# Pairs: one 512-column matmul over both halves of x1, parts added by SBUF-to-SBUF transfers, loop in written order, convolution set back

## The chip, the core and the metric

The kernel runs on one core of one Trainium2 chip. The metric is the device time of one execution in microseconds; a time is a median of runs. One profiled execution of the kernel before gives the rows below.

## What is computed

One decoder layer in fp32, sequence 512, width 2048: a token mixer (an RG-LRU group and a differential-attention group over one input projection), an output projection, a LayerNorm, and a gated MLP with a width-3 causal convolution, again with a LayerNorm. The part that the change touches is the MLP, whose up projection has 2 x 5632 columns:

```python
x = _layernorm(DEEPNORM_ALPHA * x + mix, ln_mix_g[i], ln_mix_b[i])
hu = _causal_dwconv(jnp.einsum('bsd,df->bsf', x, w_up[i]), ffn_conv_w[i], ffn_conv_b[i])
g, u = jnp.split(hu, 2, axis=-1)
ffn = jnp.einsum('bsf,fd->bsd', jax.nn.gelu(g) * u, w_down[i])
x = _layernorm(DEEPNORM_ALPHA * x + ffn, ln_ffn_g[i], ln_ffn_b[i])
```

## The kernel before

**Numbers.** Every fp32 operand of a large product is split into a high and a low fp32r part (`split`, L101 to L107: ScalarE copies the high part, L105; VectorE subtracts, L106). A product is three matmuls into one PSUM bank: weight high by x high, weight high by x low, weight low by x high (`mm3`, L109 to L114). Weights stand still, activations of 256 or 512 columns move; in w_down the hidden parts stand still and 512 columns of weights move.

**Stages.** Projections, attention and RG-LRU run to about 500 us, the output projection to 677 us. The first LayerNorm and the first four up tiles run together (`up_first`) to about 745 us: x1, the normalized input, is kept as tiles [hi | lo] of 256 + 256 columns, one for each half of the tokens and each of 16 k-tiles. Two more up tiles (i = 2, 3) are computed plainly to 797.4 us; beside them x1 is turned and stored (`turned`) and the sums of x1 for the pairs are made (`forms`, subtractions on POOL, splits on ScalarE and VectorE). Then come 40 **pairs** to 1603.6 us, then **w_down** in chunks of hidden tiles (`CHUNKS`), each added to an accumulator in SBUF, and the last chunk with the final LayerNorm.

**A pair** (class `Pair`, L772 to L873) computes one gate tile cg and one up tile cu, 128 rows by 512 tokens each, as a 2 by 2 block product with seven products instead of eight, in the order of `PRODUCTS`: p1, p5, p6, p2, p7, p3, p4. A product has 8 k-tiles and so 24 matmuls of 256 columns. p1, p6, p7 and p4 add up in bank x, p5 and p3 in y, p2 in z. The pair's steps are numbered in products from its own first one:

- `before`, steps -6 to 4: SP loads the raw weights r21, r11, r12, r22 (512 KB each); POOL issues DMAs that add another block onto r21 and r11 (`onto`, L785); VectorE makes and changes the sum s2 (L805, L816); each product's weights are split two steps ahead, into three buffers.
- `early`, steps 1 to 7: ScalarE copies a bank out (L840, L843, L845, L850, L855), VectorE adds a bank onto what was copied (L847, L852, L853).
- `late`, steps 6 to 12: `tap` (ScalarE, L759), `conv` (VectorE, L753), Gelu (L867), the product of gate and up (L871) and the store of the hidden tile to `hidd` in DRAM, which w_down loads back as `hid`.

**Order.** The loop at L931 calls for each product k the steps early, before, late and product of all pairs that are due; the Tile scheduler then orders the instructions of each engine by priority and readiness as it sees them. Each engine runs its own queue in order; DMAs wait on the queue of the engine that issues them (SP for loads and stores, POOL for the adding ones). Large tiles (x1, forms, kept weights, cg, cu, accumulators, hid) share one pool of 62 buffers of 128 x 512 (`A_BUFS`); conv and sq tiles have 12 (`T_BUFS`), raws 6.

Of the kernel before, what the change touches and what calls it, by code (L numbers as in the profile page):

```python
# [16 lines left out]
P = 128  # L17
# [7 lines left out]
QB = S // P  # L25
DFF = 5632
FT = DFF // P
CHUNKS = [20, 20, 4]
ALPHA = 2.0 ** 0.25
LN_EPS = 1e-5  # L30
RMS_EPS = 1e-5
# [14 lines left out]
NC_ = C_LQ + 4 * DH  # L46


A_BUFS = 62
T_BUFS = 12  # L50
RAW_BUFS = 3
RAW_UP = 6
# [19 lines left out]
def f32(ap):  # L72
    return ap.bitcast(F32)
# [3 lines left out]
def trunk_kernel(ctx, tc, xT, w_qkg, w_v, gate_w, w_out0, w_out, w_up0, w_up, w_down, ln2, consts, out):  # L77
# [202 lines left out]
    def v_proj(n):  # L280
        pv = [bank() for _ in range(QB)]
        if n == 0:
            load_x(0)
            W.load(1)
            load_x(1)
            W.load(2)
            load_x(2)
            load_x(3)
            W.load(3)
        for unit in range(KT // 2):  # L290
            if n == 0:
                x[2 * unit] = split(x[2 * unit])
            parts = W.take()
            if n + unit == 0:
                parts += W.take()
            if n == 0:
                x[2 * unit + 1] = split(x[2 * unit + 1])
                load_x(2 * unit + 4)
                load_x(2 * unit + 5)
            for i in range(2):  # L300
                kt = 2 * unit + i
                for tt in range(QB):
                    xs = [z[:, tt * P : (tt + 1) * P] for z in x[kt]]
                    mm3(pv[tt], xs, parts[i], kt == 0, kt == KT - 1)
                tick(4 * TK)
            if n == 0 and unit == 0:
                nc.sync.dma_start(cst, consts)
            if n == 0 and unit == 4:
                constants()
        for tt in range(QB):  # L310
            vt[tt] = split(pv[tt])

    def proj():

# [305 lines left out]
    for dt in range(KT):  # L620

        if dt == 3:
            W.hold = True
        if W.hold and not W.raws:
            assert not side
            early.close()
            W.pool = ctx.enter_context(tc.tile_pool(name="rawu", bufs=1))
            W.bufs, W.hold = RAW_UP, False
            W.load()
        xr = t_tile(F32, "xr")  # L630
        nc.sync.dma_start(xr, xT[dt])
        xrs.append(xr)
        if dt == 0:
            continue
        if dt == 1:
            pair = [bank(), bank()]
            for u in range(KT // 4):
                parts = W.take()
                for kk in range(4):
                    i = 4 * u + kk  # L640
                    tick(2 * TK)
                    assert ms[i] is not None
                    hi, lo = parts[kk // 2]
                    for o in range(2):
                        c = slice((kk % 2 * 2 + o) * P, (kk % 2 * 2 + o + 1) * P)
                        mm3(pair[o], (hi[:, c], lo[:, c]), ms[i], i == 0, i == KT - 1)
            for o in range(2):
                residual(o, pair[o])
            continue
        if dt >= KT - 2:  # L650
            wl.append([W.take(), W.take()])
            ys.append(a_tile(F32, "y"))
# [66 lines left out]
    def forms(j):  # L719
        a, b = ys[j], ys[j + KT // 2]  # L720
        sub = nc.gpsimd.tensor_tensor
        t14, t23 = t_tile(F32, "t14"), t_tile(F32, "t23")
        (t1, t4), (t2, t3) = sides(t14), sides(t23)
        (b11, b12), (b21, b22) = sides(a), sides(b)
        sub(t1, b12, b11, ALU.subtract)
        sub(t2, t1, b22, ALU.subtract)
        sub(t4, t2, b21, ALU.add)
        sub(t3, b22, b12, ALU.subtract)
        h14, l14 = a_tile(F32R, "hi"), a_tile(F32R, "lo")
        nc.scalar.activation(h14, t14, AF.Copy, scale=-1.0)  # L730
        nc.vector.scalar_tensor_tensor(l14, t14, -1.0, f32(h14), ALU.mult, ALU.subtract)
        h23, l23 = split(t23)
        form["p1", j], form["p2", j] = sides(x1[j][0]), sides(x1[j + KT // 2][0])
        form["p3", j] = sides(x1[j + KT // 2][1])
        form["p5", j], form["p4", j] = zip(sides(h14), sides(l14))
        form["p6", j], form["p7", j] = zip(sides(h23), sides(l23))

    def turned(kt):

# [32 lines left out]
    class Pair:  # L772
# [61 lines left out]

        def early(self, at):
            copy, add = nc.scalar.activation, nc.vector.tensor_tensor
            a, b = slice(0, HALF), slice(HALF, S)
            if at == 1:
                self.cg = a_tile(F32, "cg")
                copy(self.cg[:, a], self.x, AF.Copy)  # L840
            elif at == 2:
                self.p5 = t_tile(F32, "p5")[:, :HALF]
                copy(self.p5, self.y, AF.Copy)  # L843
            elif at == 3:
                copy(self.cg[:, b], self.x, AF.Copy)  # L845
            elif at == 4:
                add(self.cg[:, a], self.cg[:, a], self.z, ALU.add)  # L847
            elif at == 5:
                self.cu = a_tile(F32, "cu")
                copy(self.cu[:, b], self.x, AF.Copy, scale=-1.0)  # L850
            elif at == 6:
                add(self.cg[:, b], self.cg[:, b], self.y, ALU.add)  # L852
                add(self.cu[:, b], self.cu[:, b], self.p5, ALU.subtract)  # L853
            elif at == 7:
                copy(self.cu[:, a], self.x, AF.Copy, scale=-1.0)  # L855

        def late(self, at):
            if at == 6:
                self.g = tap(self.cg, 2 * self.i)
                conv(self.g, self.cg, 2 * self.i, 1)  # L860
            elif at == 7:
                conv(self.g, self.cg, 2 * self.i, 2)
                self.u = tap(self.cu, 2 * self.i + 1)
            elif at == 8:
                conv(self.u, self.cu, 2 * self.i + 1, 1)
            elif at == 9:
                nc.scalar.activation(self.g, self.g, AF.Gelu_apprx_tanh)  # L867
            elif at == 10:
                conv(self.u, self.cu, 2 * self.i + 1, 2)
            elif at == 11:  # L870
                nc.vector.tensor_tensor(self.g, self.g, self.u, ALU.mult)  # L871
            elif at == 12:
                nc.sync.dma_start(hidd[self.i], self.g)  # L873

    pairs = [Pair(i) for i in range(PLAIN, FT)]
# [53 lines left out]
            hid[i] = split(t)  # L929

    last = NP * len(pairs)  # L931
    for k in range(last):
        step(k, "early", 1, 8)
        step(k, "before", -6, 5)
        step(k, "late", 6, 13)
        step(k, "product", 0, NP)
        ready({last - 5: 4, last - 3: 12, last - 2: 16}.get(k, 0))
        if k == last - 4:
            W.load()
    for k in range(last, last + 6):  # L940
        step(k, "early", 1, 8)
        step(k, "late", 6, 13)

    acc = {}
    at = 0
# [28 lines left out]
        at += n  # L974


    ready(FT)
    for tt in range(QB):
        tok = slice(tt * P, (tt + 1) * P)
# [14 lines left out]
        os = []  # L994
        for fb in range(NF):
            y = acc[tt, fb]
            sq = t_tile(F32, "sq")
            nc.scalar.activation(
                sq, y, AF.Square, bias=nmean, accum_out=square[:, fb : fb + 1]
            )  # L1000
            os.append(a_tile(F32, "o"))
# [94 lines left out]
```

## Time and profile before

| | |
|---|---|
| median of 3 runs | 2094.55 us (2094.19 to 2094.75) |
| profiled execution, its own time | 2095.22 us |
| its span, first to last instruction | 2093.4 us |
| mean granted TensorE clock | 0.996 of full speed |
| busy share of the span: TensorE, VectorE, ScalarE, POOL | 99%, 62%, 48%, 9% |
| the 40 pairs | 797.4 to 1603.6 us, 20.16 us each |

The span is what the trace covers; the execution's own time is 1.8 us longer. A row of the page's engine part gives busy us, share of the span and number of instructions. Matmuls are pipelined, so their records overlap: their pace is the distance of starts. PE is TensorE, PEld its weight loads, DVE VectorE, ACT ScalarE, POOL GpSimd, SP the engine that issues most DMAs.

### The profile page before, as it was taken

The numbers are of one execution on the slowest core, as the hardware profiler recorded it, in microseconds if no ns is written. First come the engines' busy times: TensorE is split into PE (matmuls) and PEld (weight loads), VectorE is DVE, ScalarE is ACT, GpSimd is POOL, SyncE is SP. The second block draws the span as 40 slices with busy tenths as digits, with TensorE's granted clock in tenths as the row PEclk, the third lists the DMA queues.
The fourth block names the chain that finished last, engine by engine and source line by source line (L and its number), as shares of the span: only waits on it lengthen the run. The fifth ranks groups of instructions, "written<-read, shape, count | busy, mean of one in ns | idle before, by whom it ended". The sixth has DMA issues, their size and how long they took to land.

```text
span 2093.4 us, 32163 instructions
## 1 busy us (share of the span) xinstructions
PE 2075.2 (99%) x12889; PEld 1876.3 (90%) x12889; DVE 1303.3 (62%) x1963; ACT 997.2 (48%) x1635; POOL 182.5 (9%) x227
## 2 busy tenths in 40 slices
PE   9999999999999999999999999999999999999997
PEld 7888888888888899999999999999999888888886
DVE  6566645777334957777777777787778323422346
ACT  4475736667223745555555555555556222322232
POOL 1000000000222233010110100101010000000000
PEclk9999999999999999999999999999999999999999
DMA  6222222222433246666656666666667723522222
GB/s 218 96 78 89 81 91 76 86 91 92 152 114 126 94 124 165 173 170 174 171 164 174 168 174 171 165 175 166 172 172 255 257 92 114 171 91 101 96 95 81
DMA packets 98166, 288.72 MB, mean 138 GB/s; under 512 B 10208, under 2 KB 18400, under 8 KB 98016
## 3 DMA queue, kind: packets, MB, share of 16 engines
q1 hardware_dynamic: 86496, 244.71, 34.2%
q0 software_dynamic: 11520, 41.95, 11.1%
q8 instruction: 101, 1.65, 0.3%
q14 instruction: 49, 0.40, 0.1%
HBM read 266.70 MB, written 19.92 MB: 137 GB/s over the span
## 4 chain that ended last, share of the span: by engine, by line
PE 95%; ACT 3%; DVE 2%; issue 0%; DMA 0%; DVEq 0%; SPq 0%; ACTq 0%
PE ps L112 93%; PE ps L341 1%; PE ps L342 0%; ACT gt L450 0%; PE ps L743 0%; DVE y L603 0%; PE ps L371 0%; ACT s L353 0%; ACT a L456 0%; ACT L468 0%; ACT L456 0%; ACT L450 0%; ACT L353 0%; DVE hh L472 0%; ACT gt L458 0%
## 5 line engine op out<-in xcount | busy, mean ns | idle before, releaser
L105 ACT ACTIVATE whi<-raw 128x512 fp32r<-128x512 f32 (+1 forms) x676 | 528.1, 804 | 836.8 <-PE ps L112 747.8
L106 DVE TENSOR_TENSOR wlo<-raw,whi 128x512 fp32r<-128x512 f32 (+1 forms) x676 | 606.8, 915 | 474.9 <-ACT whi L105 472.5
L112 PE MATMUL ps<-hi,whi 128*128 128x256 f32 (+1 forms) x2048 | 661.2, 323 | 0.0
L112 PE MATMUL ps<-hi,wlo 128*128 128x256 f32 (+1 forms) x2048 | 658.9, 322 | 1.2 <-DVE wlo L106 1.2
L112 PE MATMUL ps<-lo,whi 128*128 128x256 f32 (+1 forms) x2048 | 658.4, 322 | 0.0
L112 PEld LDWEIGHTS ps<-hi,wlo 128*128 128x128 f32 x2048 | 390.1, 190 | 31.2 <-DVE wlo L106 2.4
L112 PEld LDWEIGHTS ps<-hi,whi 128*128 128x128 f32 x2048 | 390.1, 190 | 27.8 <-ACT cu L850 0.3
L112 PEld LDWEIGHTS ps<-lo,whi 128*128 128x128 f32 x2048 | 390.2, 191 | 27.5 <-issue 0.2
L112 PE MATMUL ps<-x,whi 128*128 128x256 f32 x2176 | 398.0, 283 | 0.0
L112 PEld LDWEIGHTS ps<-x,whi 128*128 128x128 f32 x2176 | 339.5, 192 | 0.0
L112 PE MATMUL ps<-x,wlo 128*128 128x256 f32 x1088 | 307.9, 283 | 0.0
L112 PE MATMUL ps<-whi,hi 128*128 128x512 f32 x768 | 299.6, 390 | 0.1
L112 PE MATMUL ps<-wlo,hi 128*128 128x512 f32 x768 | 299.4, 390 | 0.0
L112 PE MATMUL ps<-whi,lo 128*128 128x512 f32 x768 | 299.1, 390 | 0.0
L112 PEld LDWEIGHTS ps<-x,wlo 128*128 128x128 f32 x1088 | 208.8, 192 | 0.0
L112 PEld LDWEIGHTS ps<-whi,hi 128*128 128x128 f32 x768 | 144.5, 188 | 30.9 <-ACT hi L105 0.9
L112 PEld LDWEIGHTS ps<-wlo,hi 128*128 128x128 f32 x768 | 144.5, 188 | 29.9
L112 PEld LDWEIGHTS ps<-whi,lo 128*128 128x128 f32 x768 | 144.4, 188 | 29.9
L785 POOL DMA_DIRECT2D raw<-in_w_up x80 | 70.5, 1010 | 758.2 <-DMA raw<-in_w_up 637.8
L753 DVE SCALAR_TENSOR_TENSOR cv<-cg,cst,cv 128x511 f32<-128x511 f32 x80 | 59.8, 747 | 1.4
L753 DVE SCALAR_TENSOR_TENSOR cv<-cu,cst,cv 128x511 f32<-128x511 f32 x80 | 59.5, 744 | 0.0
L112 PE MATMUL ps<-x,hi 128*128 128x256 f32 x256 | 49.6, 295 | 4.6 <-DVE x L106 2.8
(196 smaller groups left out, 1768.6 us busy)
## 6 DMA issues: line engine op xcount, KB each, us to landing
raw<-in_w_up SPq DMA_DIRECT2D x176, 512.0 KB, 3.8
raw<-in_w_down SPq DMA_DIRECT2D x88, 512.0 KB, 3.3
raw<-in_w_up POOLq DMA_DIRECT2D x80, 512.0 KB, 6.3
raw<-in_w_qkg SPq DMA_DIRECT2D x64, 512.0 KB, 3.5
raw<-in_w_out SPq DMA_DIRECT2D x32, 512.0 KB, 3.6
hidd<-cv SPq DMA_DIRECT2D x44, 256.0 KB, 4.0
hid<-hidd SPq DMA_DIRECT2D x44, 256.0 KB, 5.6
raw<-in_w_v SPq DMA_DIRECT2D x15, 512.0 KB, 4.5
```

What stands on the lines that cost most here:

```text
L105: nc.scalar.activation(hi, src, AF.Copy)
L106: nc.vector.tensor_tensor(lo, src, f32(hi), ALU.subtract)
L112: nc.tensor.matmul(ps, a, b, start=first and n == 0, stop=last and n == 2, skip_group_check=onto)
L341: nc.tensor.matmul(ps[:, :L], qs, k[c][:, :L], start=True, stop=False)
L753: nc.vector.scalar_tensor_tensor(t[:, d:], src[:, : S - d], col(C_FW + 3 * ti + 2 - d), t[:, d:], ALU.mult, ALU.add)
L785: nc.gpsimd.dma_start(self.raw[name], w_up[2 * (self.i - 2) + g][:, n * 1024 : (n + 1) * 1024], accum_op=ALU.add,)
```

## The change

- **Products.** `mm2` replaces `mm3` in the pairs: one matmul of the high weight over the whole tile [hi | lo], 512 columns into the whole bank, and one of the low weight over hi, 256 columns into the bank's first half; on a product's last k-tile in the other order. A bank so holds two parts, which are yet to be added.
- **Results.** The copies and adds of `early` cover both parts (128 x 2 x 256). cg and cu are tiles of 128 x 1024 from a ring of 4 (`c_tile`), and POOL issues one DMA for each that adds its second half onto the first, SBUF to SBUF, 256 KB.
- **Late steps** move from 6 to 12 to 10 to 18.
- **Order.** The loop stands under `tc.manual_schedule()`, which keeps the written order on every engine, and the calls are early, late, before, product.
- **Forms.** Each product gets its own tile [hi | lo]; the splits are of 256 columns, 8 instead of 4 for each j.
- **Buffers.** `A_BUFS` 62 to 56, `CHUNKS` [20, 20, 4] to [12, 12, 16, 4]; the lo parts of v, the last two y and the final LayerNorm's o move to other pools.

```diff
-CHUNKS = [20, 20, 4]
+CHUNKS = [12, 12, 16, 4]
-A_BUFS = 62
+A_BUFS = 56
+    def c_tile(name):
+        return W.pool.tile([P, 2 * S], F32, tag="c", bufs=4, name=name)
+    def mm2(ps, w, x, first, last, onto=False):
+        n = ps.shape[-1] // 2
+        steps = [(ps, w[0], x), (ps[:, :n], w[1], x[:, :n])]
+        for k, (o, a, b) in enumerate(reversed(steps) if last else steps):
+            nc.tensor.matmul(
+                o, a, b, start=first and k == 0, stop=last and k == 1, skip_group_check=onto
+            )
...
-        h14, l14 = a_tile(F32R, "hi"), a_tile(F32R, "lo")
-        nc.scalar.activation(h14, t14, AF.Copy, scale=-1.0)
-        nc.vector.scalar_tensor_tensor(l14, t14, -1.0, f32(h14), ALU.mult, ALU.subtract)
-        h23, l23 = split(t23)
...
+        for name, t in (("p5", t1), ("p4", t4)):
+            z = form[name, j] = a_tile(F32R, "hl")
+            hi, lo = sides(z)
+            nc.scalar.activation(hi, t, AF.Copy, scale=-1.0)
+            nc.vector.scalar_tensor_tensor(lo, t, -1.0, f32(hi), ALU.mult, ALU.subtract)
+        for name, t in (("p6", t2), ("p7", t3)):
+            form[name, j] = a_tile(F32R, "hl")
+            split(t, *sides(form[name, j]))
...
-                self.x, self.y, self.z = [bank()[:, :HALF] for _ in range(3)]
+                self.x, self.y, self.z = bank(), bank(), bank()
...
-                mm3(ps, (hi[:, c], lo[:, c]), form[name, j], new and j == 0, j == n - 1, not new)
+                mm2(ps, (hi[:, c], lo[:, c]), form[name, j], new and j == 0, j == n - 1, not new)
...
             elif at == 6:
-                add(self.cg[:, b], self.cg[:, b], self.y, ALU.add)
-                add(self.cu[:, b], self.cu[:, b], self.p5, ALU.subtract)
+                add(self.g2[:, :, b], self.g2[:, :, b], y, ALU.add)
+                nc.gpsimd.dma_start(self.cg[:, :S], self.cg[:, S:], accum_op=ALU.add)
+                add(self.u2[:, :, b], self.u2[:, :, b], self.p5, ALU.subtract)
             elif at == 7:
-                copy(self.cu[:, a], self.x, AF.Copy, scale=-1.0)
+                copy(self.u2[:, :, a], x, AF.Copy, scale=-1.0)
+                nc.gpsimd.dma_start(self.cu[:, :S], self.cu[:, S:], accum_op=ALU.add)
 
         def late(self, at):
-            if at == 6:
-                self.g = tap(self.cg, 2 * self.i)
+            if at == 10:
+                self.g = tap(self.cg[:, :S], 2 * self.i)
+            elif at == 11:
                 conv(self.g, self.cg, 2 * self.i, 1)
...
-    for k in range(last):
-        step(k, "early", 1, 8)
-        step(k, "before", -6, 5)
-        step(k, "late", 6, 13)
-        step(k, "product", 0, NP)
...
+    with tc.manual_schedule():
+        for k in range(last):
+            step(k, "early", 1, 8)
+            step(k, "late", 10, 19)
+            step(k, "before", -6, 5)
+            step(k, "product", 0, NP)
+            ready({last - 5: 4, last - 3: 12, last - 2: 16}.get(k, 0))
```

What the instructions of three engines look like in their queues follows; line numbers of the changed kernel are its own.

TensorE, the start of a p5 product, before (hi and lo are the parts of a form, whi and wlo those of the weight, ps the bank):

```order
L112 MATMUL ps_16233<-hi_6700,whi_16191 128x256
L112 MATMUL ps_16233<-lo_6701,whi_16191 128x256
L112 MATMUL ps_16233<-hi_6700,wlo_16192 128x256
L112 MATMUL ps_16233<-hi_6786,whi_16191 128x256
L112 MATMUL ps_16233<-lo_6787,whi_16191 128x256
L112 MATMUL ps_16233<-hi_6786,wlo_16192 128x256
```

TensorE, the same place in a pair of the changed kernel, from the end of p1 on (hl is the form's tile of both parts):

```order
L125 MATMUL ps_12586<-x1_6472,wlo_12607 128x256
L125 MATMUL ps_12586<-x1_6472,whi_12606 128x512
L125 MATMUL ps_12584<-hl_6708,whi_12632 128x512
L125 MATMUL ps_12584<-hl_6708,wlo_12633 128x256
L125 MATMUL ps_12584<-hl_6798,whi_12632 128x512
L125 MATMUL ps_12584<-hl_6798,wlo_12633 128x256
```

Two matmuls stand where three stood, and the last k-tile of a product ends with its wide one.

VectorE, from one r21 + r11 sum (L805) on, before (wlo is a weight's low part, cv a convolution's tile):

```order
L805 TENSOR_TENSOR raw<-raw 128x1024
L106 TENSOR_TENSOR wlo<-raw,whi 128x1024
L847 TENSOR_TENSOR cg<-cg,ps 128x256
L106 TENSOR_TENSOR wlo<-raw,whi 128x1024 x2
L853 TENSOR_TENSOR cu<-cu,p_12315 128x256
L852 TENSOR_TENSOR cg<-cg,ps 128x256
L106 TENSOR_TENSOR wlo<-raw,whi 128x1024
L753 SCALAR_TENSOR_TENSOR cv<-cg,cst,cv 128x511
L753 SCALAR_TENSOR_TENSOR cv<-cg,cst,cv 128x510
L106 TENSOR_TENSOR wlo<-raw,whi 128x1024
L816 TENSOR_TENSOR raw<-raw 128x1024
L753 SCALAR_TENSOR_TENSOR cv<-cu,cst,cv 128x511
```

VectorE, the same place in the changed kernel (L823 is that sum, L109 the low part, L771 the convolution):

```order
L823 TENSOR_TENSOR raw<-raw 128x1024
L875 TENSOR_TENSOR cg<-cg,ps 128x2x256
L877 TENSOR_TENSOR cu<-cu,p_11189 128x2x256
L109 TENSOR_TENSOR wlo<-raw,whi 128x1024
L771 SCALAR_TENSOR_TENSOR cv<-cu,cst,cv 128x511
L109 TENSOR_TENSOR wlo<-raw,whi 128x1024
L771 SCALAR_TENSOR_TENSOR cv<-cu,cst,cv 128x510
L109 TENSOR_TENSOR wlo<-raw,whi 128x1024
L834 TENSOR_TENSOR raw<-raw 128x1024
L109 TENSOR_TENSOR wlo<-raw,whi 128x1024
L897 TENSOR_TENSOR cv<-cv 128x512
```

The convolution of cu (L771) that stands behind the adds onto cg and cu is now that of the pair before, with weight splits between.

POOL, two pairs of the changed kernel (L803 is the adding load that was L785; before, POOL's queue held only rows of L785 in the pairs):

```order
L876 DMA cg<-cg 128x512
L880 DMA cu<-cu 128x512
L803 DMA raw<-in_w_up 128x1024 x2
L876 DMA cg<-cg 128x512
L880 DMA cu<-cu 128x512
L803 DMA raw<-in_w_up 128x1024 x2
```

The transfers of cg and cu stand between a pair's r11 and the next r21.

## Rows read from the trace of the kernel before

**Rows 1.** The page: busy time, share of the span and instructions; the chain by engine.
```profile
PE 2075.2 (99%) x12889; PEld 1876.3 (90%) x12889; DVE 1303.3 (62%) x1963; ACT 997.2 (48%) x1635; POOL 182.5 (9%) x227
...
PE 95%; ACT 3%; DVE 2%; issue 0%; DMA 0%; DVEq 0%; SPq 0%; ACTq 0%
```

**Rows 2.** The chain in order of time: start us, us, what.
```profile
697.00 3.37 DVE y L603 x5
...
797.37 1285.29 PE ps L112 x8832
```

**Rows 3.** PE's timeline in a pair: start us, duration us, instruction.
```profile
999.75 0.28 PE L112 MATMUL ps<-x,wlo 128*128 128x256 f32 x1
999.87 0.40 PE L112 MATMUL ps<-x,whi 128*128 128x256 f32 x2
1000.11 0.28 PE L112 MATMUL ps<-x,wlo 128*128 128x256 f32 x1
```

**Rows 4.** Windows: us busy (x started) of each engine, PEclk, DMA share, GB/s.
```profile
1000.00:1100.00 100.00, 100.00 (x836) 100.00 (x835) 77.18 (x85) 52.70 (x75) 8.74 (x10) 1.00 0.64 170
...
1700.00:1800.00 100.00, 100.00 (x443) 82.81 (x442) 35.87 (x55) 27.60 (x48) 0.00 (x0) 1.00 0.39 125
```

**Rows 5.** PE's timeline in w_down: start us, duration us, instruction.
```profile
1849.91 0.39 PE L112 MATMUL ps<-whi,hi 128*128 128x512 f32 x1
...
1850.82 0.39 PE L112 MATMUL ps<-wlo,hi 128*128 128x512 f32 x1
```

**Rows 6.** Groups by form, 820 to 1590 us, then 1620 to 2050, then 744 to 797: busy us, mean ns.
```profile
L106 DVE TENSOR_TENSOR wlo<-raw,whi 128x1024 fp32r<-128x1024 f32 x267 | 326.9, 1224 | 130.9 <-ACT whi L105 129.8
...
L816 DVE TENSOR_TENSOR raw<-raw 128x1024 f32<-128x1024 f32 x39 | 47.8, 1225 | 1.3
...
L753 DVE SCALAR_TENSOR_TENSOR cv<-cu,cst,cv 128x511 f32<-128x511 f32 x39 | 29.0, 745 | 0.0
...
L871 DVE TENSOR_TENSOR cv<-cv 128x512 f32<-128x512 f32 x39 | 27.0, 692 | 1.3
...
L847 DVE TENSOR_TENSOR cg<-cg,ps 128x256 f32<-128x256 f32 x38 | 16.0, 422 | 25.9 <-PE ps L112 25.9
...
L853 DVE TENSOR_TENSOR cu<-cu,p 128x256 f32<-128x256 f32 x38 | 15.9, 418 | 0.0
L840 ACT ACTIVATE cg<-ps 128x256 f32<-128x256 f32 x39 | 14.3, 366 | 0.0
...
L967 DVE TENSOR_TENSOR acc<-acc,ps 128x512 f32<-128x512 f32 x32 | 21.6, 687 | 13.6 <-PE ps L112 13.6
...
L745 ACT ACTIVATE x1t<-ps 128x512 f32<-128x512 f32 x14 | 7.6, 584 | 0.0
```

**Rows 7.** POOL's timeline, 1190 to 1262 us: start us, us, instruction, idle before.
```profile
1197.32 1.75 POOL L785 DMA_DIRECT2D raw<-in_w_up  x2 [18.41 <-DMA raw<-in_w_up]
...
1257.80 0.86 POOL L785 DMA_DIRECT2D raw<-in_w_up  x1 [18.41 <-DMA raw<-in_w_up]
1259.31 0.86 POOL L785 DMA_DIRECT2D raw<-in_w_up  x1 [0.65 <-issue]
```

**Rows 8.** DMAs of 900 to 1560 us: line 785's landing; its queue's packets, MB, share of 16 engines.
```profile
DMA to landing us min/median/max: 5.0/7.1/10.3
...
q0 software_dynamic: 9331, 33.96, 28.6%
```

**Rows 9.** Timelines of ScalarE and VectorE at the start of the pairs.
```profile
798.99 0.64 ACT L730 ACTIVATE hi<-t 128x512 fp32r<-128x512 f32 x1
...
800.22 0.69 DVE L731 SCALAR_TENSOR_TENSOR lo<-t,hi 128x512 fp32r<-128x512 f32 x1
...
801.49 0.68 DVE L106 TENSOR_TENSOR lo<-t,hi 128x512 fp32r<-128x512 f32 x1
```

**Rows 10.** What PE's weight loads waited for, 690 to 2080 us: us, times, longest.
```profile
PEld ps L112 <- ACT cu L850: 0.3, 1, 0.3
```

**Rows 11.** Groups by form on VectorE, 677 to 709 us: busy us, mean ns.
```profile
L106 DVE TENSOR_TENSOR lo<-raw,hi 128x512 fp32r<-128x512 f32 x9 | 6.7, 744 | 0.0
```

More of the change, by code (lines that the diff above doesn't have):

```diff
@@ L310, in v_proj @@
         for tt in range(QB):
-            vt[tt] = split(pv[tt])
+            vl = att.tile([P, S], F32R, tag="vl", bufs=6, name="vl")
+            vt[tt] = split(pv[tt], lo=vl)
     def proj():
@@ L651, in trunk_kernel @@
             wl.append([W.take(), W.take()])
-            ys.append(a_tile(F32, "y"))
+            if dt == KT - 2:
+                last2 = c_tile("y")
+            ys.append(last2[:, :S] if dt == KT - 2 else last2[:, S:])
             continue
@@ L728, in forms @@
         sub(t3, b22, b12, ALU.subtract)
-        h14, l14 = a_tile(F32R, "hi"), a_tile(F32R, "lo")
-        nc.scalar.activation(h14, t14, AF.Copy, scale=-1.0)
-        nc.vector.scalar_tensor_tensor(l14, t14, -1.0, f32(h14), ALU.mult, ALU.subtract)
-        h23, l23 = split(t23)
[L733 to L736, printed above, removed]
+        form["p1", j], form["p2", j] = x1[j][0], x1[j + KT // 2][0]
+        form["p3", j] = x1[j + KT // 2][1]
+        for name, t in (("p5", t1), ("p4", t4)):
[6 more added lines that the diff above has]
+            split(t, *sides(form[name, j]))
     def turned(kt):
@@ L832, in product @@
                 c = slice(j * P, (j + 1) * P)
-                mm3(ps, (hi[:, c], lo[:, c]), form[name, j], new and j == 0, j == n - 1, not new)
+                mm2(ps, (hi[:, c], lo[:, c]), form[name, j], new and j == 0, j == n - 1, not new)
         def early(self, at):
+            two = lambda z: z.rearrange("p (z t) -> p z t", z=2)
             copy, add = nc.scalar.activation, nc.vector.tensor_tensor
             a, b = slice(0, HALF), slice(HALF, S)
+            x, y, z = [two(k) for k in (self.x, self.y, self.z)]
@@ L838, in early @@
             if at == 1:
-                self.cg = a_tile(F32, "cg")
-                copy(self.cg[:, a], self.x, AF.Copy)
+                self.cg = c_tile("cg")
+                self.g2 = two(self.cg)
+                copy(self.g2[:, :, a], x, AF.Copy)
             elif at == 2:
-                self.p5 = t_tile(F32, "p5")[:, :HALF]
-                copy(self.p5, self.y, AF.Copy)
+                self.p5 = two(t_tile(F32, "p5"))
+                copy(self.p5, y, AF.Copy)
             elif at == 3:
-                copy(self.cg[:, b], self.x, AF.Copy)
+                copy(self.g2[:, :, b], x, AF.Copy)
@@ L846, in early @@
             elif at == 4:
-                add(self.cg[:, a], self.cg[:, a], self.z, ALU.add)
+                add(self.g2[:, :, a], self.g2[:, :, a], z, ALU.add)
             elif at == 5:
-                self.cu = a_tile(F32, "cu")
-                copy(self.cu[:, b], self.x, AF.Copy, scale=-1.0)
+                self.cu = c_tile("cu")
+                self.u2 = two(self.cu)
+                copy(self.u2[:, :, b], x, AF.Copy, scale=-1.0)
             elif at == 6:
-                add(self.cg[:, b], self.cg[:, b], self.y, ALU.add)
@@ L857, in late @@
         def late(self, at):
-            if at == 6:
-                self.g = tap(self.cg, 2 * self.i)
+            if at == 10:
+                self.g = tap(self.cg[:, :S], 2 * self.i)
+            elif at == 11:
                 conv(self.g, self.cg, 2 * self.i, 1)
-            elif at == 7:
+            elif at == 12:
                 conv(self.g, self.cg, 2 * self.i, 2)
-                self.u = tap(self.cu, 2 * self.i + 1)
-            elif at == 8:
+            elif at == 13:
+                nc.scalar.activation(self.g, self.g, AF.Gelu_apprx_tanh)
+                self.u = tap(self.cu[:, :S], 2 * self.i + 1)
+            elif at == 14:
@@ L865, in late @@
                 conv(self.u, self.cu, 2 * self.i + 1, 1)
-            elif at == 9:
-                nc.scalar.activation(self.g, self.g, AF.Gelu_apprx_tanh)
-            elif at == 10:
+            elif at == 15:
                 conv(self.u, self.cu, 2 * self.i + 1, 2)
-            elif at == 11:
+            elif at == 17:
                 nc.vector.tensor_tensor(self.g, self.g, self.u, ALU.mult)
-            elif at == 12:
+            elif at == 18:
                 nc.sync.dma_start(hidd[self.i], self.g)
@@ L931, in trunk_kernel @@
     last = NP * len(pairs)
-    for k in range(last):
-        step(k, "early", 1, 8)
-        step(k, "before", -6, 5)
-        step(k, "late", 6, 13)
-        step(k, "product", 0, NP)
[L937 to L940, printed above, removed]
-        step(k, "early", 1, 8)
-        step(k, "late", 6, 13)
+    with tc.manual_schedule():
[5 more added lines that the diff above has]
+            ready({last - 5: 4, last - 3: 12, last - 2: 16}.get(k, 0))
+            if k == last - 4:
+                W.load()
+    for k in range(last, last + 12):
+        step(k, "early", 1, 8)
+        step(k, "late", 10, 19)
     acc = {}
@@ L974, in trunk_kernel, with split2 @@
         at += n
+    def split2(z):
+        return z[:, :S], z[:, S:]
     ready(FT)
@@ L993, in trunk_kernel @@
         nc.vector.tensor_scalar_mul(nmean, nmean, -1.0 / D)
-        os = []
+        os = [z for _ in range(NF // 2) for z in split2(c_tile("o"))]
         for fb in range(NF):
@@ L1000, in trunk_kernel @@
             )
-            os.append(a_tile(F32, "o"))
             nc.vector.scalar_tensor_tensor(os[fb], y, nmean, gb[0][fb], ALU.add, ALU.mult)
```

## The prediction

> **What bounds the kernel now.** Read the page's first part first: TensorE is busy for 99% of the span and carries 95% of the chain that ended last [rows 1]. Busy matmuls overlap in the records, so that share alone does not prove a limit. The chain in order of time does: from 797.37 us one unbroken piece of 8832 matmuls runs for 1285 us, through all pairs and nearly all of w_down, and ahead of it the stretch around the first LayerNorm has VectorE pieces [rows 2]. So in the pairs the time is the number of matmuls times the pace at which they start. For the pace read the timeline, starts and not durations (a 283 ns record overlaps the next two): three 256-column matmuls of one k-tile take 1000.11 - 999.75 = 0.36 us [rows 3]. The windows confirm it: 836 start in 100 us, one per 0.1197 us, while w_down's 512-column ones come 443 in 100 us, one per 0.226 us, both at clock 1.00 [rows 4]; 1850.82 - 1849.91 is four of these, 0.2275 us each [rows 5]. I take 0.120 and 0.2264 us (1285.29 us = 6720 x 0.120 + 2112 x 0.2264 + 0.7 fits both). Next to TensorE, VectorE is at 77% and ScalarE at 53% in this stretch [rows 4].
>
> **The products.** Per pair, product and k-tile, 40 x 7 x 8 = 2240 times, three 256-column matmuls become one of 512 and one of 256. The first moving tile holds [hi|lo], so the columns are the same 768. By the rows: before 3 x 0.120 = 0.360 us, after 0.2264 + 0.120 = 0.3464 us, a gain of 13.6 ns, and 2240 x 13.6 ns = **-30.5 us**, all of it on the path. A pair goes from 20.16 to 19.40 us, a product from 2.88 to 2.77 us. What no row shows is a 256 behind a 512 with another weight. Bounds: at the 256's price per column the triple stays at 0.360 (gain 0); at the 512's price per column it is 1.5 x 0.2264 = 0.3396 (gain 45.7 us). I take the sum of the two rows, since both leave the same 13 ns over columns / 2.4 GHz (106.7 and 213.3 ns), so that the excess goes by the matmul. The Trainium skill, page "TensorE: Matmul & The Clock Gate", section "Wait — 56ns, not 53.3ns?", speaks against so much: it gives a warm matmul only about 2.5 ns over its columns, by which one matmul fewer would be worth 2240 x 2.5 ns = 5.6 us; the trace disagrees, with 13 ns at both widths.
>
> **Work added beside it.** Three VectorE adds per pair go from 256 to 512 columns: 422, 422 and 418 ns become about 687, 687 and 692 ns (the widest analogues) [rows 6], +0.80 us. Five ScalarE copies go from 366 to 584 ns, +1.09 us [rows 6]. VectorE then has 0.77 x 20.16 + 0.80 = 16.4 us per 19.40 us (84%), ScalarE 0.53 x 20.16 + 1.09 = 11.7 us (60%). In totals both stay covered by TensorE; if the cover went, they would cost up to 40 x 1.9 = 76 us. The bank's reuse is the closest edge: p1, p6, p7 and p4 add up in one bank, and each is copied out (0.58 us now) during the one product, 2.77 us, that stands before the next of them. In-order VectorE: the heaviest step is one convolution, one weight split and one sum of raws, 0.745 + 1.224 + 1.225 = 3.19 us [rows 6], 0.42 us over a product; the weights are split two steps ahead in three buffers, and the steps beside it are lighter. Priced at 0.
>
> **The added transfers.** cg's and cu's parts are added by two SBUF-to-SBUF accumulations of 256 KB per pair, on the software queue that today carries two of 512 KB. They stand on POOL's queue behind r11's and ahead of r21's. POOL waits most of the time now, its two issues come together every 20.16 us [rows 7], so issuing two more (0.86 us each, [rows 7]) is free. What waits for them: cg's tap at step 10, issued a little after step 6 begins, so about 10 us later; cu's at step 13, some 14 us after step 7's copy. Those taps stand on ScalarE ahead of weight splits, so a late transfer becomes a late split and then a TensorE wait. Today's 512 KB ones land in 5.0 to 10.3 us, median 7.1 [rows 8]; no row shows one from SBUF. Bounds for its price: nothing if it lands within 10 us, 2 to 3 us per pair if the queue overflows (second rival). I take nothing, as half the bytes should land no later than the median of the larger ones. r11's accumulation is issued 3.25 us before a pair begins (1197.32 against 797.37 + 20 x 20.16 = 1200.57 us [rows 2, 7]) and is read by p7's split at step 2, so it has 3.25 + 2 x 2.77 = 8.8 us; it is then the first of its burst, and the split has some 2 us of margin more. By the 16 engines' time there is room: 28.6% of them are taken by the software queue now [rows 8]; all DMA is at 64% [rows 4], which grows to about (0.64 x 20.16 + 0.5 x 0.286 x 20.16) / 19.40 = 0.81 when 512 KB more per pair cost as much per byte.
>
> **Set-back convolution, written order.** The late steps move 4 to 6 products back. Only hidd's store comes later, and nothing reads it in the loop. SP's store now stands behind the next pair's r11 and r12 loads, which do not wait longer. Priced at 0 in the loop.
>
> **Ends of the pair stage, and the norm.** At the start the last forms come just in time: hi ends at 799.63, lo of the same tile at 800.91 us, and 802.17 for the other [rows 9], with p5 starting at 800.25 and reaching its last k-tile some 2.5 us later. Eight operations of 256 instead of four of 512 there put 0 to 2 us at risk. At the end p4's copy stands behind reloads of hid; today TensorE loses 0.3 us there [rows 10]; I allow 0 to 5. I take +1.5 us for both. With 56 instead of 62 large buffers, two or three kept weights' splits (0.74 us each on VectorE) [rows 11] fall later, into the serial stretch at 677 to 705 us where VectorE is on the chain [rows 2]: 0 to +4, taken +2. CHUNKS [12,12,16,4] adds 16 accumulator adds of 0.687 us in w_down, where VectorE is at 36% [rows 4, 6]: 0. The attention part and the last LayerNorm keep their operations: 0.
>
> **Sum.** -30.5 + 1.5 + 2 = -27.0 us. The profiled execution took 2095.2 us, 0.67 above the median of 2094.55, so 2094.55 - 27.0 = 2067.6; I say **2068 us**.
>
> **Rivals.**
> 1. *VectorE or ScalarE runs late in written order (0.11).* The loop no longer lets a scheduler put a ready split ahead of a waiting one. For it: 84% and a 3.19 us step. Against: totals fit, buffers are two steps deep. If the excess of one step, 0.42 us, is lost once per pair: 40 x 0.42 = 17 us back, about 2085 us.
> 2. *The software queue overflows (0.13), the other side.* Its two transfers are issued 1.51 us apart [rows 7]; if the first lands after 5.0 and the median lies midway, the second ends 1.51 + 2 x (7.1 - 5.0) = 5.7 us behind it [rows 8]. If a 256 KB accumulation within SBUF also takes 5.7 us (it moves as many rows, reads and writes SBUF, and shares the ports), four take 22.8 us a pair, against 20.16 today: 40 x 2.64 = +106 us, about 2200. It decides at (19.40 - 11.4) / 2 = 4.0 us for one; at half price, 2.85 us, they fit (17.1 us). Against: half the bytes, and no HBM end. The Trainium skill's fit ("DMA: Bandwidth & Descriptors", section "Anatomy of one DMA — SWDGE (gpsimd) path") of 2.0 us plus bytes / 436e3 would give 2.6 us, an estimate; nothing here has measured it.
> 3. *The excess is not per matmul (0.04 and 0.03).* If a smaller matmul count is worth only a fixed few ns, 5.6 us of gain less 3.5 leaves about 2092 at most and 2089 if the ends cost nothing; if a 256 behind a 512 pays the 512's extra again, 0.360 us, there is no gain and 2098. Against: both rows' 13 ns.
> 4. *More than one excess goes (0.03)*: 0.3396 us per triple, 2052 us.
>
> **How the numbers follow.** Forecast 0.66 (its own range 2061 to 2080: no loss at the ends, or all bounds of them), rival 1 0.11, rival 2 0.13, rival 3 0.07, rival 4 0.03. A measurement of this kernel tells about 0.2% (4.2 us) from no change. Faster: 0.66 + 0.08 of rival 1 + 0.04 + 0.03 = 0.81; same: 0.03 + 0.02 of rival 1 = 0.05; slower: 0.13 + 0.01 = 0.14. The range 2061 to 2093 holds the forecast, most of rival 1 and the small gain: about 0.8.
>
> **What would show it.** In the profile after: 40 pairs of 19.40 us (windows with some 577 matmuls in 100 us: 200 / 0.3464), TensorE unbroken through them, VectorE near 84% there, cg's transfers landing under 10 us, few DVE waits at the norm. Wrong: a TensorE wait on a weight split once per pair (rivals 1, 2; the split's own wait tells which: on a DMA or on VectorE), or 0.36 us per k-tile (rival 3).

## The result and the profile after

| | before | after |
|---|---|---|
| median | 2094.37 us (2093.60 to 2094.75, 4 runs) | 2077.75 us (2076.77 to 2079.83, 4 runs) |
| profiled execution, its own time | 2095.22 us | 2076.77 us |
| its span | 2093.4 us | 2075.0 us |
| a pair | 20.16 us | 19.74 us |

The ratio is 0.9922, with a 95% interval of 0.9905 to 0.9940: 16.6 us less where 27 were forecast. The direction and the mechanism are as forecast, the size is not. The profile after shows at once where the missing 10 us are not: no engine got in TensorE's way.

The page's engine part and its chain, answering to [rows 1]:

```profile
PE 2055.9 (99%) x10649; PEld 1755.3 (85%) x10649; DVE 1324.5 (64%) x1995; ACT 1042.2 (50%) x1651; POOL 253.0 (12%) x307
...
PE 94%; ACT 3%; DVE 2%; issue 0%; DMA 0%; DVEq 0%; SPq 0%; ACTq 0%
```

2240 matmuls are gone (12889 to 10649), as the change says. The chain in order of time, answering to [rows 2]:

```profile
698.07 3.47 DVE y L617 x4
...
795.89 786.70 PE ps L125 x4464
1582.59 7.50 PE ps L115 x33
...
1592.87 471.26 PE ps L115 x2079
```

From 795.89 us on it is TensorE alone again: the pairs (L125), the first matmuls of w_down ahead of the last product, and w_down. All that TensorE waited for between 690 and 2080 us (us in total, times, longest) lies in `up_first`, at the LayerNorm:

```profile
PE ps L115 <- DVE x L109: 2.5, 1, 2.5
PE ps L115 <- ACT x L108: 2.4, 1, 2.4
```

So neither the stall of written order nor an overflowing queue took place. What is left is the pace. TensorE's timeline in the pairs (start us, duration us, instruction), two neighbouring products of eight k-tiles, answering to [rows 3]:

```profile
1100.21 0.40 PE L125 MATMUL ps<-x,whi 128*128 128x512 f32 x1
1100.44 0.28 PE L125 MATMUL ps<-x,wlo 128*128 128x256 f32 x1
1100.56 0.40 PE L125 MATMUL ps<-x,whi 128*128 128x512 f32 x1
1100.79 0.28 PE L125 MATMUL ps<-x,wlo 128*128 128x256 f32 x1
1100.91 0.40 PE L125 MATMUL ps<-x,whi 128*128 128x512 f32 x1
...
1103.03 0.40 PE L125 MATMUL ps<-hl,whi 128*128 128x512 f32 x1
...
1105.85 0.40 PE L125 MATMUL ps<-x,whi 128*128 128x512 f32 x1
```

A product takes 1103.03 - 1100.21 = 2.82 us, and so does the next, 1105.85 - 1103.03. Eight wide matmuls at the pace that w_down still has (471.26 us for 2079 in the chain above, 0.2267 each) and eight narrow ones at the pace of before would be 8 x 0.2267 + 8 x 0.120 = 2.773 us. On average over 900 to 1500 us the next matmul starts 0.235 us after a wide one and 0.117 us after a narrow one. The rest of the profile sits where the forecast put it; the windows (us busy and instructions of PE, PEld, DVE, ACT, POOL; clock, DMA share, GB/s) answer to [rows 4]:

```profile
1000.00:1100.00 100.00, 100.00 (x570) 87.05 (x569) 79.42 (x87) 59.30 (x76) 17.64 (x20) 1.00 0.80 200
...
1700.00:1800.00 100.00, 100.00 (x443) 82.84 (x442) 36.87 (x57) 25.37 (x45) 0.00 (x0) 1.00 0.37 116
```

VectorE is at 79% (forecast 84% of a shorter pair), ScalarE at 59% (60%), DMA at 0.80 (0.81), and w_down runs at its old pace. The counts of a window include what only reaches into it, two or three matmuls here, so the timeline is the better measure of pace; the 570 themselves would already have shown a miss against the 577 forecast.

POOL's timeline shows the burst of a pair, answering to [rows 7]. Behind it stand, answering to [rows 8], the landings of cg's transfer (line 876) and of cu's (line 880) by the views of these lines, and the software queue's packets, MB and share of the 16 engines, all of 900 to 1560 us:

```profile
1209.24 0.87 POOL L803 DMA_DIRECT2D raw<-in_w_up  x1 [15.94 <-DVE raw L823]
1209.78 1.23 POOL L876 DMA_DIRECT2D cg<-cg  x1
1211.28 0.86 POOL L880 DMA_DIRECT2D cu<-cu  x1 [0.28 <-ACT cu L879]
1211.81 1.22 POOL L803 DMA_DIRECT2D raw<-in_w_up  x1
```

```profile
DMA to landing us min/median/max: 7.0/7.6/8.5
...
DMA to landing us min/median/max: 6.1/7.7/8.9
```

```profile
q0 software_dynamic: 19331, 52.74, 45.4%
```

Four transfers leave within 2.6 us, and those of cg and cu land 7.0 to 8.5 and 6.1 to 8.9 us later, well above the 2.6 us of the estimate in rival 2, but in time: cg's tap began at 1219.34 us, 9.6 us after the transfer's issue, so about 1 us was to spare. By the share of the engines a transfer within SBUF takes (0.454 x 19.74 - 0.286 x 20.16) / 2 = 1.6 us of all 16 engines, against 0.286 x 20.16 / 2 = 2.9 us for one of 512 KB from DRAM.

### The profile page after: what moved, and what is told of

It is laid out like the page before. It is cut to its first block, busy times and chain, and to the rows that moved or that the text cites. A ratio compares the mean times of both kernels' runs of the same rounds, so it can differ in the third digit from the quotient of the medians.

```text
span 2075.0 us, 27944 instructions
## 1 busy us (share of the span) xinstructions
PE 2055.9 (99%) x10649; PEld 1755.3 (85%) x10649; DVE 1324.5 (64%) x1995; ACT 1042.2 (50%) x1651; POOL 253.0 (12%) x307
## 4 chain that ended last, share of the span: by engine, by line
PE 94%; ACT 3%; DVE 2%; issue 0%; DMA 0%; DVEq 0%; SPq 0%; ACTq 0%
PE ps L115 54%; PE ps L125 38%; PE ps L355 1%; ACT gt L464 0%; PE ps L356 0%; PE ps L761 0%; ACT s L367 0%; PE ps L385 0%; DVE y L617 0%; ACT a L470 0%; ACT L482 0%; ACT L470 0%; ACT L464 0%; ACT L367 0%; DVE hh L486 0%
## 5 line engine op out<-in xcount | busy, mean ns | idle before, releaser
L109 DVE TENSOR_TENSOR wlo<-raw,whi 128x512 fp32r<-128x512 f32 (+1 forms) x676 | 605.9, 914 | 478.1 <-ACT whi L108 476.5
L125 PE MATMUL ps<-hl,whi 128*128 128x512 f32 x1280 | 458.9, 398 | 0.0
L125 PE MATMUL ps<-x,whi 128*128 128x512 f32 x960 | 349.2, 398 | 0.0
L125 PE MATMUL ps<-hl,wlo 128*128 128x256 f32 x1280 | 333.5, 281 | 0.0
L115 PE MATMUL ps<-hi,whi 128*128 128x512 f32 (+1 forms) x768 | 299.0, 389 | 0.0
L115 PE MATMUL ps<-hi,wlo 128*128 128x512 f32 (+1 forms) x768 | 296.8, 386 | 1.2 <-DVE wlo L109 1.2
L115 PE MATMUL ps<-lo,whi 128*128 128x512 f32 (+1 forms) x768 | 296.3, 386 | 0.0
L125 PEld LDWEIGHTS ps<-hl,whi 128*128 128x128 f32 x1280 | 238.3, 188 | 43.6
L125 PEld LDWEIGHTS ps<-hl,wlo 128*128 128x128 f32 x1280 | 242.0, 189 | 14.9
L125 PE MATMUL ps<-x,wlo 128*128 128x256 f32 x960 | 250.1, 281 | 0.0
L125 PEld LDWEIGHTS ps<-x,whi 128*128 128x128 f32 x960 | 180.8, 188 | 32.6
L125 PEld LDWEIGHTS ps<-x,wlo 128*128 128x128 f32 x960 | 181.5, 189 | 11.1
L115 PEld LDWEIGHTS ps<-hi,wlo 128*128 128x128 f32 x768 | 144.4, 188 | 31.4 <-DVE wlo L109 2.4
L115 PEld LDWEIGHTS ps<-lo,whi 128*128 128x128 f32 x768 | 144.5, 188 | 27.4 <-issue 0.2
L115 PEld LDWEIGHTS ps<-hi,whi 128*128 128x128 f32 x768 | 144.5, 188 | 27.1 <-ACT whi L108 0.2
```

Of the source, the lines that this page charges most:

```text
L109: nc.vector.tensor_tensor(lo, src, f32(hi), ALU.subtract)
L115: nc.tensor.matmul(ps, a, b, start=first and n == 0, stop=last and n == 2, skip_group_check=onto)
L125: nc.tensor.matmul(o, a, b, start=first and k == 0, stop=last and k == 1, skip_group_check=onto)
```

## The experiments

A pair's time is read from one row for each kernel: the ScalarE copy that starts cg (line 840 before) runs once per pair, and the view of one line gives the count and the first and last start. Of 810 to 1560 us, first before, then after:

```profile
L840 ACT ACTIVATE cg<-ps x37: 364/365/368, 821.3 to 1547.0; 128x256 f32<-128x256 f32 x37
```

```profile
L862 ACT ACTIVATE cg<-ps x38: 597/599/599, 818.4 to 1548.8; 128x512 f32<-128x512 f32 x38
```

725.7 / 36 = 20.16 us and 730.4 / 37 = 19.74 us.

### Three matmuls of 256 again

```diff
-        steps = [(ps, w[0], x), (ps[:, :n], w[1], x[:, :n])]
+        steps = [(ps[:, :n], w[0], x[:, :n]), (ps[:, n:], w[0], x[:, n:]), (ps[:, :n], w[1], x[:, :n])]
...
```

> The changed kernel with its wide matmul undone alone: the high weight over hi into the bank's first half, over lo into the second, the low weight over hi into the first, three matmuls of 256 columns. In the profile of the changed kernel a k-tile takes 0.3525 us (a product always 2.820 us) where the rows of before gave 0.3464. Theory A, a change of width between neighbours costs time (14 changes in a product of 16 matmuls, (2.820 - 8 x 0.3467) / 14 = 3.3 ns each): no change of width is left, 0.360 us per k-tile, 20.16 us per pair, 2077.8 + 40 x 0.42 = about 2094.5 us. Theory B, the work around it (written order, transfers, wider copies) takes the 6 ns per k-tile: 0.366 us, 20.5 us per pair, about 2108 us.

2095.21 us in one run (before beside it 2094.66, median of 7). The copy's row:

```profile
L862 ACT ACTIVATE cg<-ps x37: 597/600/601, 820.3 to 1546.1; 128x512 f32<-128x512 f32 x37
```

725.8 / 36 = 20.16 us: theory A, and theory B falls. With the wide matmul undone, the whole rest of the change (transfers, wider copies, written order, chunks, buffers) costs 0.5 us against before, which is no difference. So the two matmuls in place of three are all of the gain, and the 6 ns per k-tile come from TensorE's own instructions.

### Wide ones together, narrow ones together

```diff
-                mm2(ps, (hi[:, c], lo[:, c]), form[name, j], new and j == 0, j == n - 1, not new)
...
+            wide = [(ps, hi[:, col_(j)], form[name, j]) for j in range(n)]
+            narrow = [(ps[:, :m], lo[:, col_(j)], form[name, j][:, :m]) for j in range(n)]
+            steps = wide[:-1] + narrow + wide[-1:]
...
```

> The same matmuls as the changed kernel, in another order within a product: seven of 512 columns, then the eight of 256, then the last of 512. Two changes of width per product instead of 14. Theory A: 8 x 0.2267 + 8 x 0.120 + 2 x 0.0033 = 2.780 us per product instead of 2.820, 280 x 0.040 = 11.2 us less, about 2066.5 us. Theory C, a 512-column matmul takes 0.235 us in this stretch whatever stands beside it: no change, about 2078 us.

2071.10 us (2070.43 to 2071.41), ratio to before 0.9888 (0.9872 to 0.9905). Its timeline on TensorE:

```profile
1100.60 1.12 PE L855 MATMUL ps<-x,wlo 128*128 128x256 f32 x8
1101.55 0.40 PE L855 MATMUL ps<-x,whi 128*128 128x512 f32 x1
1101.78 1.77 PE L855 MATMUL ps<-hl,whi 128*128 128x512 f32 x7
1103.39 1.12 PE L855 MATMUL ps<-hl,wlo 128*128 128x256 f32 x8
1104.34 0.40 PE L855 MATMUL ps<-hl,whi 128*128 128x512 f32 x1
1104.58 1.77 PE L855 MATMUL ps<-x,whi 128*128 128x512 f32 x7
```

and its copy's row (the copy is line 869 here):

```profile
L869 ACT ACTIVATE cg<-ps x38: 598/600/601, 819.9 to 1543.3; 128x512 f32<-128x512 f32 x38
```

A product takes 1104.58 - 1101.78 = 2.80 us, more exactly 723.4 / 37 / 7 = 2.793 (19.55 us a pair). The same matmuls in another order are 6.7 us faster by the medians and 40 x (19.74 - 19.55) = 7.6 us by the pairs, which theory C can't give. But only two thirds of the forecast 11.2 us came: 8 narrow ones take 1104.34 - 1103.39 = 0.95 us, their old pace, while the 7 wide ones take 1103.39 - 1101.78 = 1.61 us, 0.230 each. The price is thus not 3.3 ns for each change: one round trip from wide to narrow and back costs 2.793 - 2.773 = 20 ns where the groups are long, and (2.820 - 2.773) / 7 = 6.7 ns where they alternate.

### The narrow matmul in the other half of the bank

```diff
-        steps = [(ps, w[0], x), (ps[:, :n], w[1], x[:, :n])]
+        steps = [(ps, w[0], x), (ps[:, n:], w[1], x[:, :n])]
```

> As the changed kernel, but the narrow matmul (low weight over hi) goes into the bank's second half instead of the first; the halves are added up anyway. Theory A: nothing changes, 0.3525 us per k-tile, about 2078 us. Theory D, the narrow matmul and the next wide one wait for each other because both add to the first half at once: the extra 6 ns go or move, 0.3467 us per k-tile would give 2078 - 13 = about 2065 us.

2078.19 us in one run, the copy's row:

```profile
L862 ACT ACTIVATE cg<-ps x38: 598/600/602, 819.8 to 1550.2; 128x512 f32<-128x512 f32 x38
```

730.4 / 37 = 19.74 us, unchanged: theory D falls. Which columns of the bank the narrow one adds to does not matter.

### Every matmul of 512

```diff
-        steps = [(ps, w[0], x), (ps[:, :n], w[1], x[:, :n])]
+        steps = [(ps, w[0], x), (ps, w[1], x)]
```

> As the changed kernel, but the low weight too runs over the whole tile [hi | lo], 512 columns (it adds the low by low part that is left out otherwise). Theory A: no change of width is left, 2 x 0.2267 = 0.4533 us per k-tile, 3.627 us per product, 280 x (3.627 - 2.820) = 226 us more, about 2304 us. Theory C (a 512-column matmul takes 0.235 us in this stretch): 0.470 us per k-tile, 3.760 us per product, 263 us more, about 2341 us.

2303.05 us in one run, theory A to 1 us:

```profile
L862 ACT ACTIVATE cg<-ps x29: 598/598/598, 825.3 to 1536.1; 128x512 f32<-128x512 f32 x29
```

710.8 / 28 = 25.39 us for 112 matmuls of 512 columns, 0.2267 us each. With the same engines, transfers and banks at work, the wide matmul has its w_down pace (0.2267) once no narrow one stands between. High and low weights still alternate here, so it is not the change of the weight that costs. Theory C falls.

### Order turned in every other product

```diff
...
+            odd = ((self.i - PLAIN) * len(PRODUCTS) + at) % 2
+            steps = narrow + wide if odd else wide + narrow
...
```

> As e2_grouped, but a product's eight wide matmuls and its eight narrow ones stand in turned order in every other product (wide, narrow; narrow, wide; wide, narrow): one change of width per product instead of two. The last run showed that an isolated change costs more than one in a quick alternation: (2.793 - 2.773) / 2 = 10 ns. Theory A: 2.783 us per product, 280 x 0.010 = 2.8 us under the 2071.1 us of e2_grouped, about 2068 us. Theory E, the cost of 20 ns is one per product and not one per change: no difference, about 2071 us.

2067.16 us (2066.33 to 2068.28), ratio to before 0.9873 (0.9856 to 0.9889): the fastest kernel of this study, 10.6 us under the changed one and 27.0 us under before.

```profile
1099.79 2.00 PE L856 MATMUL ps<-hl,whi 128*128 128x512 f32 x8
1101.63 1.98 PE L856 MATMUL ps<-x,whi 128*128 128x512 f32 x8
1103.44 1.12 PE L856 MATMUL ps<-x,wlo 128*128 128x256 f32 x8
1104.40 1.12 PE L856 MATMUL ps<-hl,wlo 128*128 128x256 f32 x8
1105.36 0.86 PE L856 MATMUL ps<-hl,whi 128*128 128x512 f32 x3
```

Two products take 1105.36 - 1099.79 = 5.57 us, 2.785 each. The eight wide ones behind narrow ones take 1.84 us, the eight behind those 1.81, the pace of w_down. The copy's row (line 870 here) gives 740.4 / 38 = 19.48 us a pair:

```profile
L870 ACT ACTIVATE cg<-ps x39: 597/598/600, 817.9 to 1558.3; 128x512 f32<-128x512 f32 x39
```

Halving the round trips took 723.4 / 37 - 740.4 / 38 = 0.067 us off a pair, 2.7 us in all (2.8 forecast), so the cost is one of the change, not of the product: theory A, and E falls. The medians are 3.9 us apart; the rest lies ahead of the pairs, which began at 795.60 us here and at 797.47 us in the run before.

Where the cost sits, a narrower view of the same trace (1101.12 to 1103.30 us) shows, since it begins behind the fifth wide one:

```profile
1100.95 0.84 PE L856 MATMUL ps<-hl,whi 128*128 128x512 f32 x3
```

The five wide ones behind the narrow ones take 1100.95 - 1099.79 = 1.16 us, 0.232 each, the three behind them 1101.63 - 1100.95 = 0.68 us, 0.227 each. All groups of 900 to 1500 us in this run and in the one before are alike: behind narrow ones, five wide ones lose 27 ns together and the sixth has its old pace; behind wide ones, the first two narrow ones come 7.5 ns early together, so that a round trip costs the 20 ns. So not every change of width costs, as theory A has it, but only the one from narrow to wide, and it is paid over five matmuls. That fits the smaller price of an alternation: there each wide one stands behind a narrow one, takes 0.235 us like the first two of a group, and the narrow one behind it gives 3 ns back.

### Late steps back at 6 to 12

```diff
-            step(k, "late", 10, 19)
+            step(k, "late", 6, 13)
```

(with the steps of `late` numbered as before the change)

> As the changed kernel, but the late steps stand where they stood before (6 to 12) instead of 10 to 18, still in written order. The transfer of cg's parts lands 7.6 us after its issue and that of cu 7.7 us, and their taps now stand in ScalarE's queue right behind the issue, ahead of weight splits. Theory F, the set-back convolution is what hides the transfers: ScalarE waits some 7 us twice per pair, the splits made two products (5.6 us) ahead are late, TensorE loses 5 to 12 us per pair, 2280 to 2560 us. Rival: splits run far enough ahead or the waits overlap: about 2078 us.

2640.11 us in one run, above the top of theory F's range. What was waited for in 850 to 1550 us:

```profile
ACT cv L777 <- DMA cg<-cg: 199.6, 20, 10.6
...
ACT cv L777 <- DMA cu<-cu: 140.0, 21, 7.8
...
PE ps L125 <- ACT whi L108: 103.2, 21, 5.5
...
PE ps L125 <- ACT cg L862: 75.1, 20, 4.9
```

As theory F says, the taps (L777) stop ScalarE for 10 and 7 us per pair, and splits and copies behind them come late for TensorE. The window shows what the range had left out:

```profile
1000.00:1100.00 100.00, 72.93 (x332) 59.47 (x331) 47.30 (x51) 34.60 (x45) 9.89 (x12) 0.81 0.49 116
```

The granted clock is 0.81: after its waits TensorE runs part of the time at 1.2 GHz in place of 2.4. A pair took 34.1 us (22 copies from 833.5 to 1550.7), 14.4 more than after; the two waits are (103.2 + 75.1) / 20.5 pairs = 8.7 of it, and the lower clock can account for the remainder of 5.7: a mean of 0.81 is 0.19 x 34.1 x 2 = 13 us of each pair at half speed, in which up to 6.5 us are lost.

### The scheduler's order

```diff
-    with tc.manual_schedule():
+    if True:
         for k in range(last):
```

> As the changed kernel, but the scheduler orders the loop of the pairs again, as in the kernel before; the steps' numbers stay. On POOL r11's transfer then stands between cg's and cu's, on VectorE the convolutions stand elsewhere. Theory G, the written order only has to keep splits ahead and any such order does: 19.74 us per pair, about 2078 us. Rival: the scheduler, which puts cg's convolution and tap where it takes the transfer to have landed, lets ScalarE or VectorE wait on it once per pair: 1 us each would give 2118 us.

2239.52 us in one run: the rival, and with four times its price. Waits of 850 to 1550 us:

```profile
ACT cv L777 <- DMA cu<-cu: 124.9, 30, 6.1
...
PE ps L125 <- ACT cg L867: 79.7, 28, 5.0
```

ScalarE's timeline shows the place:

```profile
1203.50 0.82 ACT L777 ACTIVATE cv<-cu,cst 128x512 f32<-128x512 f32 x1 [2.25 <-DMA cu<-cu]
1204.22 0.57 ACT L867 ACTIVATE cg<-ps 128x512 f32<-128x512 f32 x1
```

The scheduler puts cu's tap ahead of the next pair's copy out of bank x (L867). The tap waits for the transfer, the copy behind it is late, and p7 can't start on the bank. That is (23.6 - 19.74) = 3.9 us per pair (32 copies from 819.2 to 1551.4), of which the wait is 79.7 / 29.6 = 2.7; the granted clock was 0.93 in 1000 to 1100 us. So with these transfers the order that the scheduler chose costs far more than the change brings.

### VectorE adds the parts

```diff
-                nc.gpsimd.dma_start(self.cg[:, :S], self.cg[:, S:], accum_op=ALU.add)
+                add(self.cg[:, :S], self.cg[:, :S], self.cg[:, S:], ALU.add)
```

(the same for cu)

> As the changed kernel, but VectorE adds the two parts of cg and of cu (two adds of 128 x 512, 0.69 us each, per pair) in place of the two transfers. VectorE is busy 15.7 us of 19.74 per pair and would be at 17.1 (87%). Theory H, VectorE still has the room in written order: TensorE unbroken, about 2078 us. Rival, the order's heavy steps overrun a product: a wait on a weight's split per pair, 0.5 us each, about 2098 us.

2078.87 us in one run, 730.4 / 37 = 19.74 us a pair (38 copies from 820.4 to 1550.8): theory H. VectorE has the room, 85% busy:

```profile
1000.00:1100.00 100.00, 100.00 (x570) 86.91 (x568) 85.44 (x97) 59.27 (x76) 8.78 (x10) 1.00 0.67 175
```

The transfers spare VectorE 6% and cost TensorE nothing; they bring nothing either.

### Vector adds, late steps at 6 to 12

The edits of "VectorE adds the parts" and of "Late steps back at 6 to 12" together.

> Vector adds in place of the transfers, as in the run with VectorE's adds (2078.9 us), and the late steps at 6 to 12 as before the change, in written order. Theory J, the convolution is set back only for the transfers' landing: without them nothing is late, 19.74 us per pair, about 2079 us. Rival: in step 7 the copy out of the bank, VectorE's add, the tap and the split now stand one behind another on ScalarE and VectorE, and a split comes late: 0.5 to 1 us per pair, 2099 to 2119 us.

2129.99 us in one run, somewhat past the rival's range; theory J falls. Waits of 850 to 1550 us:

```profile
ACT cv L777 <- DVE cg L877: 139.6, 33, 4.2
...
PEld ps L125 <- DVE wlo L109: 40.5, 66, 0.6
```

Without any transfer, cg's tap still holds ScalarE for 4.2 us in each pair, until VectorE has come to its add; two weight splits per pair are 0.6 us late, and the pair takes 21.03 us (36 copies from 823.8 to 1559.9). The granted clock stayed at 1.00 over 800 to 1550 us. The set-back is not for the transfers alone: in written order whatever stands at the front of ScalarE's queue must be ready when its turn comes.

### The kernel before once more

> The kernel before once more, for a second profile. In the first one TensorE's granted clock in 700 to 711 us, behind the LayerNorm's idle stretch, is 0.53 of full speed on average, in the profiles of the changed kernel and of its variants 0.69; the pairs began 1.5 us earlier after the change although the forecast had put 2 us of loss there. Theory I, the shorter low stretch is the change's own: 0.53 again here. Rival: it falls by chance: about 0.69 here, with the pairs starting about 1.5 us earlier than 797.4 us; about 2093 to 2095 us either way.

2094.78 us in one run. The window of 700 to 711 us, first as in the first profile of before, then in this one:

```profile
700.00:711.00 11.00, 7.88 (x36) 7.58 (x37) 11.00 (x21) 8.80 (x21) 5.16 (x6) 0.53 0.13 48
```

```profile
700.00:711.00 11.00, 7.39 (x40) 7.19 (x41) 11.00 (x21) 8.80 (x21) 5.12 (x6) 0.69 0.13 48
```

The same kernel had 0.53 and then 0.69, so the rival holds: around the LayerNorm's idle stretch the clock falls from 2.4 to 1.2 GHz for a time that differs between executions of one kernel (two were profiled). The pairs began at 796.91 us here, 0.5 us earlier than before's first profile, and not 1.5.

## Why the prediction was right, and where it was not

**Right in kind.** What was forecast was a gain on TensorE's path alone, hidden additions, no stall. All three hold, and 2077.75 us lies in the range. That it also lies in the forecast's own 2061 to 2080 is in part luck: the bounds named there (ends 0 to 5 and 0 to 2, norm 0 to 4) add up to 2064 to 2075 only, and the true triple with the ends and the norm as taken would have given 2094.4 - 16.8 + 3.5 = 2081. Two errors partly cancelled.

**The step that failed is the triple's price.** "By the rows: before 3 x 0.120 = 0.360 us, after 0.2264 + 0.120 = 0.3464 us." It measured 2.820 / 8 = 0.3525 us: a gain of 7.5 ns, 2240 x 7.5 = 16.8 us in place of 30.5 (0.2264 itself was 0.3 ns low, worth 0.7 us). The paragraph went on that no row showed a 256 behind a 512 and gave bounds of 0.3396 and 0.360; the value lies inside, on the dear side of the sum taken. The ground for the choice, "the excess goes by the matmul", holds only among neighbours of one width: uniform streams have 13 ns over columns / 2.4 GHz at both widths (20.16 us a pair with all narrow, 25.39 with all wide), mixed ones pay more, on the wide matmuls behind a narrow one. Wide and narrow grouped brought back 7.6 us in the pairs, turned groups 10.3 (6.7 and 10.6 by the medians). What inside TensorE makes the step from narrow to wide cost is not settled: the half of the bank is ruled out, and so is the change between high and low weights, which the run of 512 alone has too. Each matmul has a weight load of its own (as many PEld as PE in the page), so no run here tells whether the 13 ns belong to the matmul or to its load, nor whether the loads play a part in the extra.

**The page's rule.** By the 2.5 ns of the Trainium skill ("TensorE: Matmul & The Clock Gate", section "Wait — 56ns, not 53.3ns?") the gain would have been 5.6 us, an estimate; it was 16.6, and the excess over the columns is 13 ns in both uniform streams here. The measurement decides.

**The ends and the norm.** Taken +1.5 and +2, they cost nothing to be seen: no wait of TensorE at either end of the pairs, and matmuls after the LayerNorm went on at 708.70 us (708.84 and 708.80 in the two profiles of before). The pairs began 1.5 us earlier than in before's first profile, which with 16.8 makes the profiled executions' 18.45 us but for 0.15. Before's two profiles are 0.5 us apart there, and the pairs of the changed kernel and its variants, whose code up to the pairs is the same, began anywhere between 795.6 and 798.6 us: 1.5 us is within that scatter. The medians, 16.6 us apart, fit the pairs alone.

**Work beside it, and the transfers.** Priced at 0, and 0 it was (0.5 us with the wide matmul undone). Rival 2 asked whether a transfer takes more than 4.0 us of the queue: its share of the engines is 1.6 us, and landings stay under 9 us. One step there was off without a cost: r11's accumulation leaves 1.2 us before a pair (1209.24 against 795.89 + 21 x 19.74 = 1210.43), not 3.25, since POOL waits for VectorE's sum (L823) first. Rival 1, written order, was argued from the wrong side: the written order doesn't cost; the scheduler's order costs 162 us, and written order without the set-back 562.

**Rival 3** (the excess is not per matmul) held in part: a 256 and a 512 side by side do pay extra, 6 ns, somewhat under half of the 13 ns that the saved matmul gave.

## What to carry to other kernels

Where TensorE bounds, each matmul saved by a wider one was worth up to 13 ns here, and most of it only where equal widths stood together: 7.5 ns in alternation, 10.9 in groups, 12.1 in turned groups. So order a product as all wide, then all narrow, and turn the order in the next one. A pace read from uniform streams is a bound for a mixed one, not its price. In a written order, an operation that waits for a transfer or another engine belongs as many steps later as that takes, since everything behind it on its engine waits too, and a TensorE that waits may also be granted half its clock for part of the time (0.81 on average in the run without the set-back).

## What the runs showed of the hardware

- Matmuls of mixed widths cost time: 20 ns for a round trip between groups of eight, 6.7 ns in quick alternation, by products of 2.793 and 2.820 us against 2.773. The price lies on the first five wide ones behind a narrow one (0.232 us each, then 0.227), not on the step from wide to narrow.
- The cost does not depend on the bank's half, nor, as far as was tried, on the transfers: products take 2.82 us with DMA at 0.80 and, with vector adds, at 0.67.
- Short waits in every pair brought the granted clock to 0.93 (2.7 us of waits in 23.6) and 0.81 (8.7 in 34.1), so that the loss was well above the waits; with two waits of 0.6 us in 21.0 it stayed at 1.00.
